# A DiT block with gated attention and 32 experts: unread products at the start, a reordered opening and attention step, smaller last transfers

## The chip, the cores and the metric

The kernel runs on one core of one Trainium2 chip. The metric is the device time of one launch in microseconds, as the median of several runs. Every operand and result is 32-bit float; a matrix product of such operands is two instructions on TensorE, a transposition is one.

## The reference

One transformer block over 256 tokens of width 1024, with 256 context tokens:

```python
sh1, sc1, g1, sh2, sc2, g2 = split(silu(c) @ w_mod + b_mod, 6)
h  = rms_norm(x, norm1_g) * (1 + sc1) + sh1          # and the same for ctx: keys and values only
k_a, v_a, k_b, v_b, q_a, q_b, g_a, g_b = split(h @ w_in)
y_a = global_attn(rope(q_a), [k_a, k_ctx], [v_a, v_ctx])
y_b = window_attn(rope(q_b), [k_b, k_ctx], [v_b, v_ctx], sink)
x = x + g1 * ((sigmoid(g_a) * (y_a @ w_br_a) + sigmoid(g_b) * (y_b @ w_br_b)) @ w_o)
h2 = rms_norm(x, norm2_g) * (1 + sc2) + sh2
top 4 of 32 experts a token, softmax weights "combine"
x = x + g2 * sum_e combine[:, e] * (swiglu(h2 @ w_e1[e] + b_e1[e]) @ w_e2[e] + b_e2[e])
out = rms_norm(x, final_g)
```

## The kernel before

**Weights.** All weights come through one queue of transfers that SyncE issues in the order of the list `pieces` (lines 45 to 86), into a ring of slots: four areas of 4 MB (`twins`), each two areas of 2 MB, each two halves of 1 MB. `pump` (line 99) issues the next pieces as long as a slot of their size is free, strictly in the list's order, and `done` (line 141) gives a slot back when the program has written its last use; on the chip SyncE then waits for the engine that reads it. Later `grow` adds a 4 MB area (`xxp`, line 638) and a 2 MB area (`r_qt`, line 820). Expert e has 8 MB in `w1` and 4 MB in `w2`. Experts 0 to 9 (`N_ONE = 10`) and 31 are loaded in 2 MB pieces, the others in 4 MB ones. The last two experts' second matrices are loaded together by output columns (`w2l`: three pieces of 2 MB and two of 1 MB).

**Opening (lines 184 to 335).** x is held transposed, 8 blocks of 128 features by 256 tokens. VectorE and ScalarE square the blocks, and TensorE sums the squares over the features by products with `ones` into `ssp` (line 232). `m0_prod(j)` computes block j of the first two modulation vectors as a row for c and one for c_ctx, and ScalarE copies it to `msb`; `m0_turn(j)` turns it into a column and VectorE modulates block j of x with it. `crow_half(h)` spreads half of silu(c) over all partitions (`cps`, tag "y", one buffer, which `ssp` uses too) for the rest of the modulation, which VectorE (`mod_v`) or GpSimd and ScalarE (`mod_p`, `mod_a`) compute as row sums. `inv_norm` is the root on ScalarE and the reciprocal on VectorE. Then, block by block, the q products (`q_prods`, line 296) run with the remaining modulation blocks between them.

**Attention (lines 511 to 636).** Eight units u (four of either branch, each two heads), in two halves `qt` of 128 tokens. The loop at line 611 writes the order of the engines' work by hand: transposition of the probabilities of unit u (`turn`, whose copies go to ScalarE and VectorE in turn), scores and exponentials of unit u + 1 (`scores`), the pending y steps, the product of the weights with the values of unit u - 1 (`weigh`, in the first half only), half a gate block, and a row or two of the modulation. `weigh` writes y and the spread row sums in one bank with one buffer; `y_steps` copies the row sums (ScalarE, line 578) and multiplies (VectorE, line 579). The steps that `weigh(u - 1)` leaves in the first half are thus done in the second half, behind the scores.

**From attention to the experts (lines 642 to 843).** The branch products and the output projection (`wo`, eight blocks m) on TensorE, with statistics, router logits and the experts' first bias prepared beside them. ScalarE then issues two transfers: g2 spread over the partitions (512 KB from a row in memory that was written before) and the second bias `be2` (256 KB). `x1_back(tb)` brings the new x back to tokens by features by products with the identity into `acc`, in which the experts' outputs are summed later. VectorE selects the top 4 and ranks the tokens of each expert; `pick` makes the selection matrix of a pair of experts.

**Experts (lines 847 to 1013).** At most 64 tokens an expert, two experts a pair. `gather` fetches the tokens of a pair by products, `gemm1` multiplies eight row blocks k of w1, `act` and `act_turn` form the activation, `gemm2` the eight blocks of w2, `scatter` adds the pair's outputs to `acc`. The loop at line 1002 runs the first `n` row blocks of expert e + 1, then `gemm2(e)`, then the other blocks. `steps` hangs small work into `gemm1` behind a given block: the gather of the next pair behind block 3 of each odd expert.

**End (lines 1015 to 1109).** Experts 30 and 31 are finished together by column groups: `last2(c)`, `share(c - 1)`, squares and `gain`. `total(tb)` sums the squares of a half of the tokens and takes the root on ScalarE, `finish(tb)` scales on ScalarE and VectorE and issues the output.

Of the kernel before, what the change touches and what calls it, by code (L numbers as in the profile page):

```python
# [7 lines left out]
F32 = mybir.dt.float32  # L8
# [7 lines left out]
DRAM = bass.MemoryType.DRAM  # L16

NE = 32
N_ONE = 10
CAP = 64  # L20
EPS = 1e-6
ALPHA = 1.702
# [13 lines left out]
def tile_dit_block(ctx: ExitStack, tc: tile.TileContext, xcT, consts, small, rows,  # L36
# [14 lines left out]
        pieces.extend(("mod", i, w_mod[i]) for i in ids)  # L51

    def w1s(e, ks):
        if ks in ((0, 1), (2, 3)) and e >= N_ONE:
            pieces.append(("w1", (e, ks[0]), w1[e, ks[0] // 2]))
        else:
            pieces.extend(("w1", (e, k), w1[e, k // 2, :, 4096 * (k % 2):4096 * (k % 2) + 4096]) for k in ks)

    def w2s(e):
        if e < N_ONE:  # L60
            pieces.extend(("w2", (e, k), w2[e, :, 4096 * k:4096 * k + 4096]) for k in range(2))
        else:
            pieces.append(("w2", (e, 0), w2[e]))
# [11 lines left out]
    pieces.extend(("wo", i, w_o[i]) for i in range(4))  # L75
    w1s(0, range(4))
    for e in range(NE - 2):
        n = 2 if e + 1 >= N_ONE else 1
        w1s(e + 1, tuple(range(n)))
        w2s(e)  # L80
        w1s(e + 1, tuple(range(n, 4)))
# [140 lines left out]
        return f1.tile([128, 256], F32, name=name, tag="t1", bufs=5)  # L222

    ssp = ps1.tile([128, 512], F32, name="ssp", tag="y")
    for k in range(8):
        sq = t1("sq")
        v = x[:, k, :]
        if k in (0, 1, 2, 5, 7):
            nc.vector.tensor_tensor(out=sq, in0=v, in1=v, op=ALU.mult)
        else:  # L230
            nc.scalar.activation(out=sq, in_=v, func=AF.Square)
        nc.tensor.matmul(ssp[:, 0:256], ones, sq, start=(k == 0), stop=(k == 7))

    def inv_norm(ps):
        r = t1("rinv")
        nc.scalar.activation(out=r, in_=ps, func=AF.Sqrt, bias=eps, scale=1.0 / 1024)
        nc.vector.reciprocal(r, r)
        return r
# [31 lines left out]

    def crow_half(h):

        cps = ps1.tile([128, 512], F32, name="cps", tag="y")
        for b in range(4):
            nc.tensor.matmul(cps[:, 128 * b:128 * b + 128],
                             cmod[:, 4 * h + b, 0:1].to_broadcast([128, 128]), ident, start=True, stop=True)
        nc.scalar.copy(out=crow[:, 512 * h:512 * h + 512], in_=cps)

    m0_prod(0)
    rinv = inv_norm(ssp[:, 0:256])  # L280
    m0_prod(1)
    crow_half(0)
    crow_half(1)
    for k in range(8):
        v = x[:, k, :]
        (nc.gpsimd if k >= 6 else nc.vector).tensor_tensor(out=v, in0=v, in1=rinv, op=ALU.mult)
        if k in (0, 2):
            m0_turn(k // 2)

    qa = [ps1.tile([128, 4, 256], F32, name="qa", tag="s", bufs=2) for _ in range(2)]  # L290
    csq = [tanh[2 + i // 2].rearrange("p a b -> p (a b)")[:, 512 * (i % 2):512 * (i % 2) + 512] for i in range(4)]
# [318 lines left out]

    for u in range(8):
        for qt in range(2):
            turn(u, 2 * qt)
            turn(u, 2 * qt + 1)
            if u < 7:
                scores(u + 1, qt)
            y_steps()
            if u and qt == 0:
                weigh(u - 1)
            if u < 7:  # L620
                gate_half(9 + u, qt)
            else:
                for m in (2 * qt, 2 * qt + 1):
                    tag, bufs = (("mm", 1), ("s", 2))[m % 2]
                    br_prod(0, m, ps1.tile([128, 512], F32, name="mm", tag=tag, bufs=bufs))
            if u < 7:
                norm_p(u + 1, qt)
            mod_v()
            if qt == 0 and u < 7:
                mod_p()  # L630
            elif u < 7:
                mod_a()
# [96 lines left out]
    braw = t8[1]  # L729
    b1e = b1.rearrange("(e c) n -> e (c n)", c=4)  # L730
    LOW_R, MID_R, ALL_R = slice(96, 128), slice(64, 96), slice(64, 128)
    for r in (slice(0, 32), MID_R, LOW_R):
        nc.scalar.dma_start(out=braw[r, :], in_=b1e)

# [14 lines left out]
    for m in range(8):  # L749
# [15 lines left out]
            stats(*pend)  # L765
        pend = (m, zt)
        bias_parts(m)
        if m == 1:

            ws = mtx[:, 3, :].rearrange("p (k e) -> p k e", k=8)  # L770
            nc.vector.tensor_tensor(out=ws, in0=wr, in1=sh2.unsqueeze(2).to_broadcast([128, 8, 32]), op=ALU.mult)
            for n in (4, 2, 1):
                nc.vector.tensor_tensor(out=ws[:, 0:n, :], in0=ws[:, 0:n, :], in1=ws[:, n:2 * n, :], op=ALU.add)
        elif m == 2:
            lp = ps2.tile([128, 512], F32, name="lp", tag="sp", bufs=2)
            nc.tensor.matmul(lp[:, 0:32], ones, ws[:, 0, :], start=True, stop=True)
            nc.vector.tensor_tensor(out=lb, in0=lp[:, 0:32], in1=brb, op=ALU.add)
    squares(sqs)
    stats(*pend)
    nc.scalar.dma_start(out=g2, in_=g2_dram[0:1, :].to_broadcast([128, 1024]))  # L780

    x_t, y_t = t8[0].rearrange("p (a c) -> p a c", a=2), [t8[1].rearrange("p (a c) -> p a c", a=2)]
    be2 = y_t[0][:, 1, 0:512]
    nc.scalar.dma_start(out=be2, in_=b2)

    nc.scalar.activation(out=junk, in_=eps, func=AF.Exp)
    acc = {}
# [1 line left out]
    def x1_back(tb):  # L789

        for h in range(2):
            acc[tb, h] = ps2.tile([128, 512], F32, name="acc", tag=("xg", "sp")[tb], bufs=2)
            for b in range(4):
                nc.tensor.matmul(acc[tb, h][:, 128 * b:128 * b + 128], x1T[:, 4 * h + b, 128 * tb:128 * tb + 128],
                                 ident, start=(b == 0), stop=False, skip_group_check=True)

    x1_back(0)
    nc.vector.reciprocal(rt, rt)
# [82 lines left out]
    def gemm1(e, u, ks, between=None):  # L881
        p, j = divmod(e, 2)
        for k in ks:
            if e == NE - 1 and k > 5:
                w = take("l1", k - 6)
            else:
                big = ("w1", (e, 2 * (k // 4) if N_ONE <= e < NE - 1 else k // 2))
                o = 2048 * (k % 4 if N_ONE <= e < NE - 1 else k % 2)
                w = take(*big)[:, o:o + 2048]
            for ch in (0, 2, 1, 3):  # L890
                c0 = 64 * (ch // 2)
                nc.tensor.matmul(u[c0:c0 + 64, ch % 2, :], XT[p][:, k, 64 * j:64 * j + 64],  # L892
                                 w[:, 512 * ch:512 * ch + 512], start=(e == 0 and k == 0), stop=(e > 0 and k == 7))
            if e == NE - 1 and k > 5:
                done("l1", k - 6)
            elif k % (4 if N_ONE <= e < NE - 1 else 2) == (3 if N_ONE <= e < NE - 1 else 1):
                done(*big)
            if between and k in between:
                between[k]()
# [29 lines left out]
    def gemm2(e, aT):  # L929
        p, j = divmod(e, 2)  # L930
        y = ps2.tile([128, 512], F32, name="y", tag="y")
        for k in range(8):
            n = 4 if e < N_ONE else 8
            w = take("w2", (e, k // n)).rearrange("p (k c) -> p k c", k=n)[:, k % n, :]
            l = aT[:, k % 4, 64 * (k // 4):64 * (k // 4) + 64]
            for h in range(2):
# [45 lines left out]
    def steps(e):  # L982
# [9 lines left out]
                s[5] = lambda: pick(p + 1)  # L992
            return s
        if e == 1:
            return {3: lambda: gather(p + 1), 6: settle}
        return {3: lambda: gather(p + 1)}

    u0 = ps2.tile([128, 2, 512], F32, name="u", tag="u")
    gemm1(0, u0, range(8), steps(0))
# [2 lines left out]
    for e in range(NE - 2):  # L1002
# [1 line left out]
        if p:  # L1004
            scatter(p - 1, (j,))
        u = bias1(e + 1)
        n = 4 if N_ONE <= e + 1 < NE - 1 else 2
        gemm1(e + 1, u, (0,))
        aT = act_turn(e)
        gemm1(e + 1, u, range(1, n), steps(e + 1))  # L1010
# [93 lines left out]
    total(0)  # L1104
    square(3, 1, False)
    square(4, 1, False)
    finish(0)
    total(1)
    finish(1)


# [182 lines left out]
```

## Time and profile before

| | us |
|---|---|
| median of 3 runs | 1190.56 |
| lowest, highest run | 1188.13, 1192.37 |
| the profiled execution, whole | 1187.26 |
| its span in the trace | 1185.5 |
| TensorE busy | 1108.2 |
| VectorE busy | 324.8 |
| ScalarE busy | 143.6 |
| GpSimd busy | 48.0 |

Times in the trace are from the start of the span; 1.8 us of the profiled execution lie around it. 456.88 MB are read from memory, 386 GB/s over the span. TensorE's products are pipelined and their ends are modelled, so a busy TensorE is not one at its peak. The row of an engine in order of time names start, duration, engine, line, operation, output, inputs and shapes; in brackets is how long the engine stood idle before it and what released it.

### The profile page before, as it was taken

What the parts mean: (1) busy time and instruction counts of PE and PEld (TensorE: products, weight loads), DVE (VectorE), ACT (ScalarE), POOL (GpSimd) and SP (SyncE); (2) the same over time, 40 slices, a digit from 0 to 9 for tenths busy, and PEclk for the clock granted to TensorE, in tenths of its full rate; (3) what the DMA queues carried; (4) which work ended last, traced back from release to release, by engine and by line L of the source; (5) the groups of instructions that cost most, each with busy time, mean ns of one, the idle gap of its engine ahead of it and who ended that gap; (6) DMA issues with size and microseconds to landing.
All of it is one profiled execution on the core that took longest, in us unless ns stands there. A gap on an engine that the chain in (4) does not pass through costs nothing.

```text
span 1185.5 us, 13010 instructions
## 1 busy us (share of the span) xinstructions
PE 1108.2 (93%) x5610; PEld 528.0 (45%) x5610; DVE 324.8 (27%) x711; ACT 143.6 (12%) x313; POOL 48.0 (4%) x37
## 2 busy tenths in 40 slices
PE   7999999999999999999999998989898989898986
PEld 5888666894334334343333333333333333333224
DVE  3273666343222221221212112121212121212123
ACT  2122554031000000000000000000000000000002
POOL 0232100030000000000000000000000000000001
PEclk9999999999999999999999999999999999999998
DMA  9995643959999999999999999999999999999994
GB/s 377 380 399 206 221 141 143 392 181 398 429 427 429 427 428 428 427 434 431 427 435 430 427 435 431 431 431 427 434 432 428 434 427 434 431 430 432 427 425 177
DMA packets 28735, 458.83 MB, mean 387 GB/s; under 512 B 3609, under 2 KB 4001, under 8 KB 6049
## 3 DMA queue, kind: packets, MB, share of 16 engines
q1 hardware_dynamic: 26928, 454.05, 90.9%
q10 hardware_dynamic: 1744, 3.90, 1.0%
q8 instruction: 46, 0.75, 0.3%
q14 instruction: 17, 0.13, 0.0%
HBM read 456.88 MB, written 1.05 MB: 386 GB/s over the span
## 4 chain that ended last, share of the span: by engine, by line
PE 59%; DMA 34%; DVE 4%; ACT 2%; issue 1%; ACTq 0%; DVEq 0%
DMA ring<-w 27%; PE u L892 24%; PE y L937 8%; DMA xxp<-w 7%; PE mm L395 3%; PE xg L855 3%; PE qa L296 2%; PE acc L953 2%; PE o L753 2%; PE br L599 2%; ACT xxp L537 1%; PE yl L1047 1%; PE kp L385 1%; PE vp L469 1%; PE ta L925 1%; DVE st L527 1%
## 5 line engine op out<-in xcount | busy, mean ns | idle before, releaser
L892 PE MATMUL u<-ring,t 128*64 128x512 f32 x1552 | 354.0, 602 | 22.2 <-DMA ring<-w 22.1
L892 PEld LDWEIGHTS u<-ring,t 128*64 128x64 f32 x1552 | 108.2, 138 | 231.6 <-issue 193.7
L937 PE MATMUL y<-ring,tmp 128*64 128x512 f32 x768 | 169.9, 594 | 17.3 <-DMA ring<-w 11.0
L944 DVE TENSOR_TENSOR t<-y,r_kv 64x512 f32<-64x512 f32 x60 | 41.3, 688 | 334.2 <-PE y L937 333.6
L937 PEld LDWEIGHTS y<-ring,tmp 128*64 128x64 f32 x768 | 53.6, 137 | 120.9 <-issue 100.1
L892 PE MATMUL u<-xxp,t 128*64 128x512 f32 x416 | 96.9, 613 | 5.4 <-DMA xxp<-w 5.4
L909 ACT ACTIVATE tmp<-tmp 128x512 f32<-128x512 f32 (+1 forms) x33 | 20.3, 617 | 629.0 <-DVE tmp L908 629.0
L908 DVE TENSOR_SCALAR tmp<-u 128x512 f32<-128x512 f32 (+1 forms) x33 | 22.3, 675 | 227.8 <-PE u L892 215.9
L855 PEld LDWEIGHTS xg<-r_kv,r_y 128*128 128x128 f32 x512 | 58.4, 192 | 12.2 <-issue 12.2
L855 PE MATMUL xg<-r_kv,r_y 128*128 128x128 f32 x512 | 61.3, 278 | 0.0
L395 PE MATMUL mm<-xxp,ring 128*128 128x256 f32 x256 | 59.9, 385 | 0.0
L953 PE MATMUL acc<-t,r_kv 128*128 128x512 f32 x120 | 59.5, 618 | 0.0
L857 DVE TENSOR_TENSOR t<-xg,modb 128x512 f32<-128x512 f32 x32 | 22.1, 691 | 132.9 <-PE xg L855 132.9
L892 PEld LDWEIGHTS u<-xxp,t 128*64 128x64 f32 x416 | 29.3, 140 | 63.5 <-issue 53.0
L395 PEld LDWEIGHTS mm<-xxp,ring 128*128 128x128 f32 x256 | 47.3, 190 | 12.6 <-issue 5.0
L937 PE MATMUL y<-xxp,tmp 128*64 128x512 f32 x176 | 39.0, 594 | 4.7 <-DMA xxp<-w 3.1
L1071 POOL TENSOR_TENSOR ring<-ring 128x256 f32<-128x256 f32 (+1 forms) x8 | 5.1, 660 | 894.4 <-DMA ring<-rows 892.7
L953 PEld LDWEIGHTS acc<-t,r_kv 128*128 128x128 f32 x120 | 20.3, 189 | 38.7 <-issue 38.7
L296 PE MATMUL qa<-xxp,ring 128*128 128x256 f32 x128 | 30.7, 388 | 0.0
L926 ACT COPY tmp<-ta 128x512 f32<-128x512 f32 x30 | 17.6, 585 | 103.5 <-PE ta L925 103.5
L753 PE MATMUL o<-r_qt,ring 128*128 128x256 f32 x128 | 28.9, 380 | 0.0
L353 DVE SCALAR_TENSOR_TENSOR ring<-ring,crow 128x1024 f32<-128x1024 f32 x22 | 26.3, 1211 | 0.0
(237 smaller groups left out, 852.7 us busy)
## 6 DMA issues: line engine op xcount, KB each, us to landing
ring<-w SPq DMA_DIRECT2D x49, 4096.0 KB, 40.4
ring<-w SPq DMA_DIRECT2D x47, 2048.0 KB, 18.5
xxp<-w SPq DMA_DIRECT2D x13, 4096.0 KB, 40.7
xxp<-w SPq DMA_DIRECT2D x10, 2048.0 KB, 16.5
ring<-w_mod SPq DMA_DIRECT2D x16, 1024.0 KB, 10.7
r_qt<-w SPq DMA_DIRECT2D x6, 2048.0 KB, 21.5
ring<-w_in SPq DMA_DIRECT2D x10, 1024.0 KB, 8.5
ring<-w_m SPq DMA_DIRECT2D x8, 1024.0 KB, 12.4
```

What stands on the lines that cost most here:

```text
L296: nc.tensor.matmul(qa[c // 4][:, c % 4, :], w[:, 128 * c:128 * c + 128], x[:, j, :], start=(j == 0 and c % 2 == 0), stop=(j == 7), skip_gr ...
L353: nc.vector.scalar_tensor_tensor(out=w, in0=w, scalar=1.0, in1=crow, op0=ALU.mult, op1=ALU.mult, accum_out=moda[:, t:t + 1])
L395: nc.tensor.matmul(gp[0][:, 0:256], w[:, k, :], x[:, k, :], start=(k == 0), stop=(k == 7))
L599: nc.tensor.matmul(ps[:, 0:256], w[:, k, 128 * (m % 2):128 * (m % 2) + 128], Y[:, 4 * br + k, :], start=(k == 0), stop=(k == 3))
L753: nc.tensor.matmul(ps[:, 0:256], w[:, k, :], M[:, k, :], start=(k == 0), stop=(k == 7))
L855: nc.tensor.matmul(xp[:, b, :], z[:, tb, 128 * k:128 * k + 128], S[:, tb, :], start=(tb == 0), stop=(tb == 1))
L857: nc.vector.tensor_tensor(out=XT[p][:, 4 * h:4 * h + 4, :], in0=xp, in1=sh2[:, 4 * h:4 * h + 4].unsqueeze(2).to_broadcast([128, 4, 128]), ...
L892: nc.tensor.matmul(u[c0:c0 + 64, ch % 2, :], XT[p][:, k, 64 * j:64 * j + 64], w[:, 512 * ch:512 * ch + 512], start=(e == 0 and k == 0), st ...
L908: nc.vector.tensor_scalar(out=w(glu), in0=v[:, bs, 0, :], scalar1=LIMIT, scalar2=None, op0=ALU.min)
L937: nc.tensor.matmul(y[64 * h:64 * h + 64, :], l, w[:, 512 * h:512 * h + 512], start=(k == 0), stop=(k == 7))
L944: nc.vector.tensor_tensor(out=YY[p][64 * j:64 * j + 64, 512 * h:512 * h + 512], in0=y[64 * h:64 * h + 64, :], in1=g2[64 * h:64 * h + 64, 5 ...
L953: nc.tensor.matmul(acc[tb, h], t[:, tb, :], y[:, s], start=False, stop=False, skip_group_check=True)
```

## The change

It has eight parts. (1) Sixteen products of `ones` with itself, into columns of `ssp` that nobody reads, stand ahead of the sum of squares. (2) The root and the two halves of the condition's row are written ahead of the first and the second modulation block, the halves in the two banks that the q products use later (tag "s"), and block 1 is turned right behind block 0. (3) In attention the y steps stand at the head of a half instead of behind the scores. (4) g2 and `be2` are loaded behind output block 2, `be2` into a free part of `msc`. (5) `x1_back` uses transpositions instead of products with the identity. (6) The gather of the next pair stands behind row block 2 instead of 3. (7) Experts 29 to 31 are loaded in 2 MB pieces (`N_TWO = 29`), so that expert 29 and 30 have two blocks instead of four ahead of `gemm2`. (8) The second half's sum and root stand ahead of the first half's scaling.

```diff
-N_ONE = 10
+N_ONE, N_TWO = 10, 29
 ...
     def w1s(e, ks):
-        if ks in ((0, 1), (2, 3)) and e >= N_ONE:
+        if ks in ((0, 1), (2, 3)) and N_ONE <= e < N_TWO:
 ...
     def w2s(e):
-        if e < N_ONE:
+        if not N_ONE <= e < N_TWO:
 ...
-        n = 2 if e + 1 >= N_ONE else 1
+        n = 2 if N_ONE <= e + 1 < N_TWO else 1
 ...
     ssp = ps1.tile([128, 512], F32, name="ssp", tag="y")
+
+    for _ in range(16):
+        nc.tensor.matmul(ssp[:, 256:384], ones, ones, start=True, stop=True)
 ...
-        cps = ps1.tile([128, 512], F32, name="cps", tag="y")
+        cps = ps1.tile([128, 4, 256], F32, name="cps", tag="s", bufs=2).rearrange("p a b -> p (a b)")[:, 0:512]
 ...
+    rinv = inv_norm(ssp[:, 0:256])
+    crow_half(0)
     m0_prod(0)
-    rinv = inv_norm(ssp[:, 0:256])
+    crow_half(1)
     m0_prod(1)
-    crow_half(0)
-    crow_half(1)
     for k in range(8):
         v = x[:, k, :]
         (nc.gpsimd if k >= 6 else nc.vector).tensor_tensor(out=v, in0=v, in1=rinv, op=ALU.mult)
-        if k in (0, 2):
-            m0_turn(k // 2)
+        if k < 2:
+            m0_turn(k)
 ...
         for qt in range(2):
+
+            y_steps()
             turn(u, 2 * qt)
             turn(u, 2 * qt + 1)
             if u < 7:
                 scores(u + 1, qt)
-            y_steps()
 ...
+    be2 = msc[:, 1:3, :].rearrange("p a b -> p (a b)")
 ...
         bias_parts(m)
+        if m == 2:
+            nc.scalar.dma_start(out=g2, in_=g2_dram[0:1, :].to_broadcast([128, 1024]))
+
+            nc.scalar.dma_start(out=be2, in_=b2)
 ...
-    nc.scalar.dma_start(out=g2, in_=g2_dram[0:1, :].to_broadcast([128, 1024]))
-
 ...
-    be2 = y_t[0][:, 1, 0:512]
-    nc.scalar.dma_start(out=be2, in_=b2)
 ...
-                                 ident, start=(b == 0), stop=False, skip_group_check=True)
+                                 ident, start=(b == 0), stop=False, is_transpose=True, skip_group_check=True)
 ...
-                big = ("w1", (e, 2 * (k // 4) if N_ONE <= e < NE - 1 else k // 2))
+                big = ("w1", (e, 2 * (k // 4) if N_ONE <= e < N_TWO else k // 2))
 ...
-        n = 4 if N_ONE <= e + 1 < NE - 1 else 2
+        n = 4 if N_ONE <= e + 1 < N_TWO else 2
 ...
-            return {3: lambda: gather(p + 1), 6: settle}
-        return {3: lambda: gather(p + 1)}
+            return {2: lambda: gather(p + 1), 6: settle}
+        return {2: lambda: gather(p + 1)}
 ...
+    total(1)
     finish(0)
-    total(1)
     finish(1)
```

The lines left out repeat the same condition on e in `gemm1` and `gemm2`.

## Rows read from the trace of the kernel before

**Rows 1.** Table by stage: stretch, length, busy PE, PEld, DVE, ACT, POOL; clock, transfer share, GB/s.

```profile
88.00:98.00 10.00, 9.32 (x44) 7.89 (x43) 6.60 (x15) 1.58 (x3) 0.00 (x0) 1.00 0.01 2
246.00:256.00 10.00, 10.00 (x54) 8.97 (x53) 4.51 (x8) 4.35 (x7) 6.72 (x4) 1.00 0.08 34
282.00:561.00 279.00, 275.71 (x1332) 103.73 (x1328) 61.19 (x117) 15.22 (x27) 0.00 (x0) 1.00 1.01 428
561.00:1126.00 565.00, 517.98 (x2426) 191.64 (x2424) 108.59 (x210) 26.80 (x48) 0.00 (x0) 0.98 1.00 431
```

**Rows 2.** Chain of waits: start, length, what, one of its expert transfers.

```profile
561.47 39.73 DMA ring<-w
```

**Rows 3.** Table by stage for line 232 alone: TensorE's products and weight loads.

```profile
6.50:11.00 4.50, 4.41 (x10) 3.53 (x11) 1.00 1.02 430
11.00:12.60 1.60, 1.59 (x7) 1.07 (x5) 1.00 1.02 430
```

**Rows 4.** In order of time, the opening.

```profile
0.85 0.17 DVE L200 MEMSET ones<- 128x128 f32 x1 [0.85 <-PEq L1287]
...
6.59 6.01 PE L232 MATMUL ssp<-sq,ones 128*128 128x256 f32 x16 [6.59 <-DVE sq L229]
...
16.35 1.16 PE L275 MATMUL cps<-keep,cmod 128*128 128x128 f32 x8 [0.68 <-ACT crow L277]
...
19.65 1.99 PE L296 MATMUL qa<-xxp,ring 128*128 128x256 f32 x8
```

**Rows 5.** In order of time, the attention loop.

```profile
175.62 0.69 ACT L537 ACTIVATE xxp<-s,st 128x512 f32<-128x512 f32 x1 [3.09 <-DVE st L532]
...
177.45 0.43 DVE L579 TENSOR_TENSOR r_y<-y,r 128x256 f32<-128x256 f32 x1 [1.75 <-ACT r L578]
...
177.79 0.15 DVE L546 TENSOR_TENSOR st<-st 128x2 f32<-128x2 f32 x1
...
178.06 1.21 DVE L353 SCALAR_TENSOR_TENSOR ring<-ring,crow 128x1024 f32<-128x1024 f32 x1
...
181.32 0.69 ACT L537 ACTIVATE xxp<-s,st 128x512 f32<-128x512 f32 x1 [2.10 <-DVE st L532]
...
183.17 1.20 DVE L353 SCALAR_TENSOR_TENSOR ring<-ring,crow 128x1024 f32<-128x1024 f32 x1
...
196.81 1.04 PE L553 MATMUL tp<-keep,xxp 128*128 128x128 f32 x8
...
199.54 0.66 PE L569 MATMUL y<-keep,st 128*64 128x128 f32 x8 [1.69 <-DVE r_y L579]
```

**Rows 6.** In order of time, from the routing to the first gather.

```profile
269.09 2.03 PE L794 MATMUL acc<-keep,r_qt 128*128 128x128 f32 x16
...
269.59 0.98 DVE L831 TENSOR_SCALAR r_kv<-keep,rankm,rt 128x64 f32<-128x64 f32 x4
...
270.96 3.74 PE L855 MATMUL xg<-r_kv,r_y 128*128 128x128 f32 x32
```

**Rows 7.** Transfers issued at 256.69, 278.32 and 1128.91: size, us to landing.

```profile
ring<-w SPq DMA_DIRECT2D x1, 2048.0 KB, 7.1
...
ring<-w SPq DMA_DIRECT2D x1, 2048.0 KB, 8.3
...
ring<-w2l SPq DMA_DIRECT2D x1, 2048.0 KB, 34.3
```

**Rows 8.** In order of time, SyncE's and TensorE's last experts.

```profile
1128.89 7.09 PE L892 MATMUL u<-ring,t 128*64 128x512 f32 x32 [2.67 <-DMA ring<-w]
...
1128.91 5.22 SPq L135 DMA_DIRECT2D ring<-w2l  x2
...
1165.03 3.67 PE L1047 MATMUL yl<-ring,t 128*64 128x256 f32 x32
```

**Rows 9.** In order of time, the last scaling.

```profile
1177.75 0.34 DVE L1086 SCALAR_TENSOR_TENSOR ring<-ring,fin 128x128 f32<-128x128 f32 x1
...
1178.96 0.72 ACT L1083 ACTIVATE ring<-ring,fin 128x512 f32<-128x512 f32 x1 [0.29 <-DVE fin L1082]
```

More of the change, by code (lines that the diff above doesn't have):

```diff
@@ L886, in gemm1 @@
             else:
-                big = ("w1", (e, 2 * (k // 4) if N_ONE <= e < NE - 1 else k // 2))
-                o = 2048 * (k % 4 if N_ONE <= e < NE - 1 else k % 2)
+                big = ("w1", (e, 2 * (k // 4) if N_ONE <= e < N_TWO else k // 2))
+                o = 2048 * (k % 4 if N_ONE <= e < N_TWO else k % 2)
                 w = take(*big)[:, o:o + 2048]
@@ L895, in gemm1 @@
                 done("l1", k - 6)
-            elif k % (4 if N_ONE <= e < NE - 1 else 2) == (3 if N_ONE <= e < NE - 1 else 1):
+            elif k % (4 if N_ONE <= e < N_TWO else 2) == (3 if N_ONE <= e < N_TWO else 1):
                 done(*big)
@@ L932, in gemm2 @@
         for k in range(8):
-            n = 4 if e < N_ONE else 8
+            n = 8 if N_ONE <= e < N_TWO else 4
             w = take("w2", (e, k // n)).rearrange("p (k c) -> p k c", k=n)[:, k % n, :]
```

## The prediction

> **What bounds the kernel now.** I read three views first. The table by stage [rows 1] shows where the transfers stand still: between 88 and 98 us and between 246 and 256 us the DMA share is 0.01 and 0.08, because the ring is full and waits for TensorE and VectorE to free slots. From 282 us on it is 1.00 without a break, at 428 and then 431 GB/s, to the last experts. The chain of waits [rows 2] says the same of the second part: from 561 us it is made of transfers of expert weights. So the program has two halves. Before 282 us the compute chain sets the pace, and what it saves moves the whole stream earlier. After it the bytes set the pace, and there only fewer bytes in that stretch, or a shorter way from the last bytes to the end, are worth anything. The third view, in order of time, shows each edited place [rows 3 to 8].
>
> **The start.** The eight products that sum the squares begin at 6.59 us and take 6.01 us for 16 instructions; the q products need 1.99 us for eight of the same width [rows 4]. Split at 11 us, ten of them need 4.41 us and seven, one of them counted twice, 1.59 us [rows 3], 0.44 against 0.23 each: the 1.2 GHz level and then the 2.4 GHz level by the spacing, although the granted-clock column says 1.00 in both. What TensorE did before the rise is work without a gap since 6.59 us. The change puts 16 unread 128-wide products, 32 instructions, ahead. Their operand is written at 0.85 to 1.02 us [rows 4], so they start at 1.1. At the high level one costs 0.127 us (2.03 us for 16 [rows 6]), at the low one I take twice that. If the rise comes after as much work as above, 4.5 us, 18 are done by 5.6 us and 14 more take 1.8 us: they end at 7.4, and the sum of squares starts 0.8 us late but takes 4.0 instead of 6.0 (0.25 an instruction, from the q products). Gain 2.0 - 0.8 = 1.2 us. Bounds: all 32 at the low level end at 9.2 us, 2.6 us late, with nothing won back; at best the full 2.0.
>
> The order behind it: the root for rinv no longer stands behind the copy of the first modulation product on ScalarE, and the second half of the condition's row no longer waits 0.68 us for its buffer [rows 4]. The chain to the first q product at 19.65 us is otherwise the same TensorE work, so I take 0.6 us, and bounds of 0 and 0.7. The turn at k = 1 instead of 2 moves one VectorE multiplication behind it and has room. Start together: **1.8 us**, from -2.6 to 2.7.
>
> **Attention.** VectorE and ScalarE alternate there. In a half-step without y steps it is 1.85 us from the first exponential (181.32) to VectorE's modulation row (183.17); in one with them 2.44 us (175.62 to 178.06), since the copy of the row sums and the multiplication stand behind the exponentials [rows 5]. Moved to the head of the half-step they cost VectorE its 0.34 us (177.45 to the next start at 177.79; the row's 0.43 overlaps it) and no wait. So 2.44 - 1.85 - 0.34 = 0.25 us a head, six of them 1.5 us. The copy now stands ahead of the next transposition's copy on ScalarE and could stall it if the product it reads were late. It is not: that product is queued before the gate's products, and ScalarE comes to it only after two exponentials. Then TensorE's idle 1.69 us before the last-but-one weighing product at 199.54 (released by the multiplication) goes, since that multiplication is done a half-step earlier; the transpositions end at 197.85 [rows 5], and from there the chain is TensorE's own products, up to the routing. **3.2 us**, from 0 (TensorE bound at the same pace) to 6 x 0.59 + 1.69 = 5.2.
>
> **Into the experts.** The eight products that bring x1 back take 2.03 us in 16 instructions; eight transpositions of the same size take 1.04 us [rows 5, 6]. The first set lies beside VectorE's routing steps. The second ends a microsecond earlier, but the gather that follows reads the selection that VectorE ends at 270.57, against its start at 270.96 [rows 6]. **0.4 us**, bounds 0 and 1.0; late next is the selection.
>
> The two transfers (512 and 256 KB) that ScalarE issues at 267 us run beside the stream's first pieces. Moved to m = 2 they are issued while ScalarE waits for the next output block, hidden behind that block's eight products on TensorE (uncovered, only that block's square would come late, and its sums are taken one block later), and their bytes fall into the empty stretch from 246 to 256 us [rows 1]. A 2 MB piece alone lands after 7.1 us; the one issued at 278.32, behind them, after 8.3 [rows 7]. From there the stream has no break. **1.2 us**, bounds 0 and 1.8 (0.79 MB at 428 GB/s).
>
> The gather at k = 2 instead of 3 puts a product between it and the second GEMM. Both are TensorE time in the half that the bytes bound: nothing, and if that cover went, TensorE's short wait there would show in each odd expert. A freed slot comes one gather, 3.74 us [rows 6], later, against transfers issued some 40 us ahead [rows 2].
>
> **The last experts.** Expert 29's and 30's weights come as 2 MB pieces, so the last four row blocks of expert 30 needn't wait for the whole 4 MB: half of 7.09 us, 3.5 us, leaves TensorE's chain after 1128.89 [rows 8]. But the third piece of the last weights is issued at 1128.91 and lands 34.3 us later, at 1163.2 [rows 7, 8]; its product starts at 1165.03. So 1.8 us, and late next is that landing. Against it: 2 MB pieces ran at 428 GB/s, 4 MB ones at 431 [rows 1], 0.7% of 88 us (three experts of 12.6 MB), 0.6 us. **1.2 us**, from -0.6 to 3.5. The Trainium skill ("DMA: Bandwidth & Descriptors", section "Anatomy of one DMA") speaks against this part: it gives every transfer a fixed cost of some 2 us. By it, as an estimate, five more transfers would cost 10 us instead of 0.6, and the sum would be a loss of 1.3. The trace does not agree for transfers in a full queue.
>
> The second root ahead of the first scaling: between the end of the first scaling on VectorE (1178.09) and the second on ScalarE (1178.96) stand a sum, two small steps and the root [rows 9]; they move beside the first, which they push back by 0.3. **0.3 us**, bounds 0 and 0.5.
>
> **Sum:** 1.8 + 3.2 + 0.4 + 1.2 + 1.2 + 0.3 = 8.1 us. Against the profiled execution's 1187.26 that is 1179.2. The median of the runs shown is 1190.56, 3.3 above it, and the runs after are compared with such runs: **1182.5 us**. The ends of all bounds add to -3.2 and 14.7.
>
> **Rivals.** (1) The front shrinks by half: the products end no earlier than the clock's rise can pay for (0.6 left at the start) and TensorE takes VectorE's place in attention (1.0 left). Then 0.6 + 1.0 + 0.4 + 1.2 + 1.2 + 0.3 = 4.7, 1185.9. For it: apart from that one gap no row shows how far TensorE stands behind VectorE there. Against it: the gap is its longest, and it goes. Chance 0.20.
>
> (2) The stream doesn't follow the front: slots come free earlier, but the bytes from 0 to 83 us were the limit. Then 1.2 + 1.2 + 0.3 = 2.7, 1187.9, no change that counts. Against it stand the two empty stretches [rows 1], behind which any earlier start is taken up. 0.10.
>
> (3) Slower: with halved pieces the queue runs dry in the last three experts, since a piece must wait for the one small area that an earlier piece still holds. Ten pieces at 7.1 us alone [rows 7] instead of five at 9.7 (4.19 MB at 431 GB/s [rows 1]) are 22 us more: 1182.5 + 1.2 + 22 = 1205.7. It decides once a slot comes free later than what is queued lasts; transfers are issued some 40 us ahead [rows 2], so it needs a wait of that length, and a slower kernel needs 9 us of dryness. 0.04. The Trainium skill's fixed cost, of the same page and section, would act in the same place; by it alone the time would be some 1191.9 us.
>
> (4) That products without a reader are left out of the program: only 0.6 remains of the start, 1183.7, inside the forecast's spread; 0.03.
>
> **How the numbers follow.** The forecast has 0.61, for gains from 5.5 to 12. About 0.3%, 3.6 us, is what a measurement of this kernel can tell from no change. Forecast, (1) and (4) are faster: 0.84. (2) is the same, with some scatter: 0.11. Slower 0.05: (3) and what I have not seen. The range goes from the forecast's better end, 1177.0, to rival (2) at 1188.0.
>
> **What would show it.** Right: the squares' products 0.25 apart from their first, ending near 11.4; the first q product near 17.9; no wait for the multiplication before the weighing products; expert 0's first product 5.4 us earlier; the third of the last pieces landing just before its product. Wrong: a first q product after 19.6, 2.44 us still from exponential to modulation row, pauses in the transfers after 1070, or transfers whose share falls below 1.00 between 282 and 1126 us.

## The result, and the profile after

The changed kernel takes 1179.71 us (median of four runs, 1178.89 to 1181.75) against 1190.75 us (four runs): the ratio is 0.9919, with an interval of 0.9900 to 0.9939. It is faster by 0.8%, a small change but clear of that interval, 2.8 us below the forecast of 1182.5 and inside the range of 1177.0 to 1188.0. Its profiled execution, however, was its longest, 1181.75 us with a span of 1179.9, while that of before was one of the shortest, so the two traces differ by only 5.6 us. A second profile of the same kernel (label again, below) has a span of 1178.1. The first trace shows what went wrong on the way, and the second is the better measure of the parts.

The start and the attention loop in the first profile, TensorE in order of time:

```profile
1.07 5.56 PE L227 MATMUL ssp<-ones 128*128 128x128 f32 x32 [1.07 <-DVE ones L200]
6.50 3.72 PE L235 MATMUL ssp<-sq,ones 128*128 128x256 f32 x16
...
16.59 1.99 PE L299 MATMUL qa<-xxp,ring 128*128 128x256 f32 x8
...
183.14 0.66 PE L572 MATMUL y<-keep,st 128*64 128x128 f32 x8
...
192.40 0.66 PE L572 MATMUL y<-keep,st 128*64 128x128 f32 x8
...
195.07 3.29 PE L602 MATMUL mm<-r_y,ring 128*128 128x256 f32 x14 [0.28 <-ACT t L400]
```

The squares take 3.72 us instead of 6.01 and are not late, and the first q product comes 3.06 us earlier than at 19.65 [rows 4]. The y products no longer wait for VectorE's multiplication, as the one at 199.54 did for 1.69 us [rows 5]. When the output projection begins, at 226.30 instead of 233.08, the lead is 6.8 us. But the first expert's first product starts at 271.15 instead of 274.62, a lead of 3.5. Between them lies this stretch of the output projection, of the same trace:

```profile
234.58 1.96 POOL L743 CAST be<-t 32x2048 bf16<-32x2048 f32 x1 [26.41 <-DMA t<-b]
234.72 2.11 DVE L780 TENSOR_TENSOR t<-r_kv,modb 128x256 f32<-128x256 f32 x1
...
236.86 2.61 DVE L782 TENSOR_TENSOR t<-t 128x128 f32<-128x128 f32 x3
...
239.52 0.41 PE L785 MATMUL lp<-t,ones 128*128 128x32 f32 x2 [1.47 <-DVE t L782]
...
239.77 5.39 PE L758 MATMUL o<-r_qt,ring 128*128 128x256 f32 x16
```

VectorE's product of the router's weights started 0.14 us after a conversion on GpSimd and took 2.11 us, where it took 0.42 before the change. TensorE waited 1.47 us for its sums at the lp product (which only prepares the router's bias), and the 16 instructions of the next output block, 3.62 us elsewhere, took 5.39. The table by stage of the same trace (stretch, length, busy PE, PEld, DVE, ACT, POOL; granted clock, transfer share, GB/s) tells why:

```profile
239.50:240.50 1.00, 0.98 (x5) 0.87 (x6) 0.81 (x3) 0.54 (x2) 0.00 (x0) 0.86 0.28 115
240.50:242.00 1.50, 1.50 (x5) 1.19 (x4) 0.43 (x2) 1.18 (x2) 0.22 (x1) 0.50 0.49 175
242.00:245.00 3.00, 3.00 (x12) 2.50 (x11) 0.00 (x0) 0.00 (x0) 1.90 (x1) 0.73 0.49 178
```

The granted clock fell to 0.50, the 1.2 GHz level, behind the wait. The wait (1.47) and the slower products (5.39 - 3.62 = 1.77) are 3.2 of the 3.3 us by which the lead shrank (6.78 to 3.47).

The end of the first profile, in order of time:

```profile
1160.20 3.67 PE L1052 MATMUL yl<-ring,t 128*64 128x256 f32 x32 [0.20 <-DMA ring<-w2l]
...
1173.58 0.34 SPq L1093 DMA_DIRECT2D out<-ring  x1
...
1174.44 0.35 ACTq L1093 DMA_DIRECT2D out<-ring  x1
```

The third of the last weight pieces is what its product waits for, as forecast; before, the product came 1.8 us behind the landing [rows 7, 8]. The outputs leave 0.86 us apart instead of 1.58 (1178.24 and 1179.82 before).

### The profile page after: what moved, and what is told of

The parts are those of the page before. It is cut to its first block, busy times and chain, and to the rows that moved or that the text cites. A ratio compares the mean times of both kernels' runs of the same rounds, so it can differ in the third digit from the quotient of the medians.

```text
span 1179.9 us, 13059 instructions
## 1 busy us (share of the span) xinstructions
PE 1112.7 (94%) x5626; PEld 531.6 (45%) x5626; DVE 326.6 (28%) x711; ACT 143.3 (12%) x313; POOL 47.4 (4%) x37
## 4 chain that ended last, share of the span: by engine, by line
PE 61%; DMA 35%; DVE 1%; issue 1%; ACT 1%; ACTq 0%; SPq 0%; DVEq 0%
PE u L897 22%; DMA ring<-w 20%; DMA xxp<-w 9%; PE y L942 8%; PE xg L860 5%; PE mm L398 5%; DMA r_qt<-w 3%; DMA ring<-w2l 3%; PE qa L299 2%; PE acc L958 2%; PE o L758 2%; PE br L602 2%; PE s L522 1%; PE kp L388 1%; PE vp L472 1%; PE tp L556 1%
## 5 line engine op out<-in xcount | busy, mean ns | idle before, releaser
L897 PE MATMUL u<-xxp,t 128*64 128x512 f32 x400 | 94.3, 615 | 6.5 <-DMA xxp<-w 6.5
L758 PEld LDWEIGHTS o<-r_qt,ring 128*128 128x128 f32 x128 | 25.0, 199 | 3.5
```

What stands on the lines that cost most here:

```text
L758: nc.tensor.matmul(ps[:, 0:256], w[:, k, :], M[:, k, :], start=(k == 0), stop=(k == 7))
```

## The experiments

Twelve runs with eleven kernels (one of them is timed twice, and one is the changed kernel itself). Each was timed beside the kernel before, whose medians were 1188.2 to 1189.1 us in the five groups. Differences are against `ws_early`, unless another kernel is named.

**1. The changed kernel again, and the router's product one block earlier.** `again` is unchanged. `ws_early`:

```diff
-        if m == 1:
+        if m == 0:
             ws = mtx[:, 3, :].rearrange("p (k e) -> p k e", k=8)
```

> The changed kernel as it stands, for a second profile. In its first profile 3.4 us of the 6.8 us that the front had gained were gone by the end of the output projection: VectorE's product of the router's weights took 2.11 us beside GpSimd's conversion of the bias rows (0.42 us before the change), TensorE waited 1.47 us for it, and the granted clock of the next 3 us was 0.50. Theory A: which of the two engines starts first there is a matter of 0.1 us (GpSimd began 0.14 us ahead here, at the same moment before), so it can differ from one run to the next. Where it does not happen, the output projection starts and ends with the same lead, the first expert's first product comes near 268 us instead of 271.15, and the whole is near 1178.5 us. Theory B: the change causes it in every run (the lead of the front, or the two transfers now issued in the middle of this stage). Then the second profile shows the wait of about 1.5 us at the lp product again, the first expert's first product near 271, and the whole near 1180 to 1182.

> The changed kernel with VectorE's product of the router's weights and its three additions one block earlier in the output projection (block 0 instead of block 1), when GpSimd's first conversion has not begun. Theory A and B for the cause of the wait alike: no wait of TensorE at the lp product, the granted clock stays 1.00 through the stage, the lead of 6.8 us at its start is kept to its end, and the first expert's first product comes near 267.8 us. If the front's lead reaches the end one for one, the whole is 3 us below a run that has the wait (1178.5 against 1181.7). Rival (a lead gained before the experts is lost in the weight stream): the first expert's first product comes earlier and the third of the last weight pieces lands no earlier than at 1160.0, the whole stays within 1 us of the changed kernel.

`again` took 1179.65 us (1178.45 to 1179.92; ratio 0.9909, 0.9891 to 0.9928), `ws_early` 1178.58 (1178.30 to 1179.49; 0.9906, 0.9887 to 0.9924). The trace of `again` in order of time:

```profile
235.07 0.42 DVE L780 TENSOR_TENSOR t<-r_kv,modb 128x256 f32<-128x256 f32 x1
235.52 2.35 DVE L782 TENSOR_TENSOR t<-t 128x128 f32<-128x128 f32 x3
235.65 1.90 POOL L743 CAST be<-t 32x2048 bf16<-32x2048 f32 x1 [27.13 <-DMA t<-b]
...
238.24 0.31 PE L785 MATMUL lp<-t,ones 128*128 128x32 f32 x2
...
268.07 10.52 PE L897 MATMUL u<-ring,t 128*64 128x512 f32 x48
...
1157.21 3.67 PE L1052 MATMUL yl<-ring,t 128*64 128x256 f32 x32 [0.16 <-DMA ring<-w2l]
...
1171.46 0.35 ACTq L1093 DMA_DIRECT2D out<-ring  x1
```

The bias rows landed later, so GpSimd started 0.58 us behind VectorE's product instead of 0.14 ahead; TensorE did not wait, and the clock was 1.00. Theory A holds: the change does not cause the wait in every run. The two engines stood as near to each other before the change, where they began in the same hundredth of a microsecond:

```profile
241.50 0.42 DVE L771 TENSOR_TENSOR t<-r_kv,modb 128x256 f32<-128x256 f32 x1
241.50 2.16 POOL L738 CAST be<-t 32x2048 bf16<-32x2048 f32 x1 [26.55 <-DMA t<-b]
```

Which of them comes first can thus differ from run to run in either kernel; how often it is GpSimd is not shown.

In `again` the lead of 6.43 us at the output projection (226.65) is still 6.55 at the first expert and 8.36 at the last output (1179.82 to 1171.46). `ws_early` keeps its lead in the same way (1171.27); its median is 1.1 us lower, with ranges that overlap.

**2. `ws_early` a second time**, beside experiments 6 to 8.

> The version ws_early unchanged, a second time, beside the next three on the same chip. Expected if the wait at the lp product is really out of it: granted clock 1.00 through the output projection, the first expert's first product near 267.9 us, a median within 0.7 us of 1178.6. If the wait can still happen, some of the runs lie 2 to 3 us higher.

1179.37 us (1178.34 to 1181.23), the first expert at 267.77. Two of the six runs are near 1181.2: something else costs some runs 2 us, and no profile caught it. So `ws_early` removes one known wait, but that it beats the changed kernel (1179.71 and 1179.65) is not shown. The same kernel's median moved by 0.8 us from one group to the other, so below a difference of medians against `ws_early` (1178.58) is good to about that, and the traces are the better measure.

**3. Parts of the start undone, each from `ws_early`.** `no_products`, then `order_old`, then `half_products`:

```diff
-    for _ in range(16):
-        nc.tensor.matmul(ssp[:, 256:384], ones, ones, start=True, stop=True)
```

```diff
-    rinv = inv_norm(ssp[:, 0:256])
-    crow_half(0)
     m0_prod(0)
-    crow_half(1)
+    rinv = inv_norm(ssp[:, 0:256])
     m0_prod(1)
+    crow_half(0)
+    crow_half(1)
```

```diff
-    for _ in range(16):
+    for _ in range(8):
```

(`order_old` also has the row's old buffer and the second turn at k = 2.)

> The version with the router's product moved one block up (ws_early, 1178.58 us), without the 16 unread products. My theory (they bring TensorE's rise to the 2.4 GHz level forward, out of the sum of squares): the squares' 16 instructions take about 6.0 us from 6.5 instead of 3.72 from 6.64, the first q product comes about 2.4 us later than at 16.73, near 19.1, and everything after it is later by the same amount; the whole 2.0 to 2.4 us longer, near 1180.9. Rival (the gain at the start comes from the order of the work behind the squares alone): the first q product comes within 0.5 us of 16.73 and the whole does not change.

> The version ws_early with the order behind the sum of squares as it was before the change: both modulation blocks' products around the root, the condition's rows after them in the small buffer, the second turn at k = 2. My theory: the first q product comes 0.3 to 0.7 us later than at 16.73, the unread products still bring the squares' 3.72 us, and the whole is 0.6 us longer, 1179.2, at the edge of what can be told. Rival (the order is worth most of the 2.9 us that the start gained): the first q product near 19, the whole 2 us longer.

> The version ws_early with 8 unread products in place of 16. From the rows: unread instructions ran about 0.25 us apart up to some 4.1 us and 0.127 apart after it, so 16 instructions end near 4.8 us, and TensorE stands still from there to the first square at 6.6. [...] Theory B (the level falls again in the gap, as it fell to 0.50 in the output projection after 1.5 us without work): the squares take between 4.5 and 6 us, the first q product comes 0.8 to 2.3 us later than at 16.73, the whole 1179.4 to 1181.

1180.74, 1180.67 and 1180.47 us. TensorE in order of time, first in `no_products`:

```profile
6.36 6.46 PE L233 MATMUL ssp<-sq,ones 128*128 128x256 f32 x16 [6.36 <-DVE sq L230]
...
19.19 1.99 PE L297 MATMUL qa<-xxp,ring 128*128 128x256 f32 x8
```

in `order_old`:

```profile
6.51 3.72 PE L235 MATMUL ssp<-sq,ones 128*128 128x256 f32 x16
...
11.95 1.07 PE L258 MATMUL mp<-ring,cmod 128*32 128x256 f32 x16 [0.72 <-DMA ring<-w_m]
...
18.08 1.99 PE L299 MATMUL qa<-xxp,ring 128*128 128x256 f32 x8
```

and in `half_products`:

```profile
1.06 3.78 PE L227 MATMUL ssp<-ones 128*128 128x128 f32 x16 [1.06 <-DVE ones L200]
6.52 5.25 PE L235 MATMUL ssp<-sq,ones 128*128 128x256 f32 x16 [1.67 <-DVE sq L232]
...
18.14 1.99 PE L299 MATMUL qa<-xxp,ring 128*128 128x256 f32 x8
```

The unread products are worth 2.46 us (19.19 against 16.73), and the whole follows: the last output leaves 2.94 us later (1174.21 against 1171.27). Of that, 0.65 us arises between the output projection and the first expert, where the granted clock of this trace read 0.50 from 265 to 267 us. The median is 2.2 us above `ws_early`'s and 1.4 above `ws_again`'s. The order is worth 1.35 us beside the products, more than expected: with the squares done early, the old order stands for 0.72 us at the second modulation block, which has not landed yet. Its median is 2.1 us up, but its last output leaves only 1.20 us later, at 1172.47. Without the products the order is worth only what is left of the start's 2.92 us (19.65 to 16.73), 0.46.

Eight products are not enough: TensorE stands still for 1.67 us behind them and the squares take 5.25 us, so 1.41 us of the gain is lost. These are theory B's sizes, but its ground, that the level falls again in the gap, is not shown. The table of line 227 (duration of one instruction in ns: least, median, most; first and last start) says that there was nothing to fall from, first in `half_products` and then in `ws_early`:

```profile
L227 PE MATMUL ssp<-ones x16: 421/421/582, 1.1 to 4.4; 128*128 128x128 f32 x16
...
L227 PE MATMUL ssp<-ones x32: 275/275/582, 1.1 to 6.0; 128*128 128x128 f32 x32
```

None of the 16 instructions of the eight products was of the short kind that makes up most of the 32 in `ws_early`: they ended before the rise. By the spacing the rise comes at 4.0 us in `ws_early`, near 4.7 in the first profile and near 5.6 in `again`, so it differs between runs. The granted-clock column says 1.00 in all of it.

**4. The y steps behind the scores again** (`attn_old`, from `ws_early`).

```diff
-            y_steps()
             turn(u, 2 * qt)
             turn(u, 2 * qt + 1)
             if u < 7:
                 scores(u + 1, qt)
+            y_steps()
```

> The version ws_early with the steps on the attention's row sums after the scores again, not at the head of the half-step. My theory: the stretch from the first q product (16.73) to the first output projection (226.47) becomes 3.7 us longer, with the wait of 1.7 us for VectorE's multiplication before the weighing near 199 back and the rest in six half-steps of about 0.3 us each; everything after it is later by 3.7 us, the whole near 1182.3. Rival 1 (TensorE is the bound in attention in this version, the steps' place matters only at the end): 1.7 us longer, 1180.3. Rival 2 (the stream takes the lead back): the lead is lost up to the first expert, the whole within 1 us of 1178.6.

1182.38 us (1182.01 to 1183.42), 3.8 us more than `ws_early` and 3.0 more than `ws_again`. TensorE's rows of the y products with a wait, in order of time:

```profile
142.91 0.66 PE L572 MATMUL y<-keep,st 128*64 128x128 f32 x8 [1.26 <-DVE r_y L582]
153.53 0.66 PE L572 MATMUL y<-keep,st 128*64 128x128 f32 x8 [0.31 <-DVE r_y L582]
164.15 0.66 PE L572 MATMUL y<-keep,st 128*64 128x128 f32 x8 [0.23 <-DVE r_y L582]
174.96 0.66 PE L572 MATMUL y<-keep,st 128*64 128x128 f32 x8 [0.42 <-DVE r_y L582]
185.78 0.66 PE L572 MATMUL y<-keep,st 128*64 128x128 f32 x8 [0.42 <-DVE r_y L582]
196.59 0.66 PE L572 MATMUL y<-keep,st 128*64 128x128 f32 x8 [1.70 <-DVE r_y L582]
```

The output projection starts at 230.13 instead of 226.47, 3.66 us later, and the last output leaves at 1174.79 instead of 1171.27, 3.52 us later. My theory holds, and the lead arrives almost whole at the end. With the steps at the head the y products show no wait, and the chain of waits of `ws_early` and `again` runs almost over TensorE alone from 110 to 187 us, where in `before` and `attn_old` it alternates with VectorE and ScalarE: TensorE has become the bound there.

**5. g2 and `be2` transferred behind the output projection** (`g2_old`, from `ws_early`).

```diff
-        if m == 2:
-            nc.scalar.dma_start(out=g2, in_=g2_dram[0:1, :].to_broadcast([128, 1024]))
-            nc.scalar.dma_start(out=be2, in_=b2)
...
     stats(*pend)
+    nc.scalar.dma_start(out=g2, in_=g2_dram[0:1, :].to_broadcast([128, 1024]))
+    nc.scalar.dma_start(out=be2, in_=b2)
```

> The version ws_early with the two transfers of 512 and 256 KB issued after the output projection again instead of at its block 2. My theory: the front up to the first expert's first product (267.89) keeps its time, the two transfers push back the expert weights behind them, and the third of the last pieces lands 0.8 to 1.8 us later than at about 1157; the whole 1.2 us longer, near 1179.8. Rival (the stream is not full yet when they run, the bytes fit in): the third of the last pieces lands at the same time within 0.3 us, and the whole does not change.

1179.68 us (1179.12 to 1181.04), 1.1 us above `ws_early` and 0.3 above `ws_again`. The trace gives the smaller value: the third piece's product starts at 1157.49 instead of 1157.02, and 0.11 us of that is there at the first expert (268.00 against 267.89). 0.36 us is left. TensorE's table by stage (stretch, length, busy, granted clock, transfer share, GB/s) has the reason, in `g2_old`:

```profile
270.00:276.00 6.00, 6.00 (x30) 1.00 0.91 352
```

and in `ws_early`:

```profile
270.00:276.00 6.00, 6.00 (x30) 1.00 0.62 221
```

The stream waits for a slot there (SyncE issues nothing between 264.1 and 271.5 us in either trace), and the two transfers' bytes mostly run in time that is otherwise empty. The rival is nearer.

**6. The last experts in 4 MB pieces** (`pairs_old`, from `ws_early`).

```diff
-N_ONE, N_TWO = 10, 29
+N_ONE, N_TWO = 10, 31
```

> The version ws_early with the last experts' weights in 4 MB pieces again (N_TWO = 31). My theory: row blocks 4 to 7 of expert 30 wait for the whole piece, TensorE's chain after it ends later, the third of the last pieces is no longer what its product waits for (it lands about 1156.5, 0.6 us earlier by the faster pieces, and its product starts 1.8 us after that), and the whole is 1.2 us longer, near 1179.8. Rival 1 (the term was too large since landing sets the end in either version): the product of the third piece starts within 0.5 us of 1157.0, the whole unchanged. Rival 2 (2 MB pieces cost the stream more than they give): the whole shorter by 1 us.

1180.68 us (1179.80 to 1182.90), 1.3 us above `ws_again` in the same group: the theory's size. In order of time, and then its table by stage:

```profile
1122.35 8.57 PE L897 MATMUL u<-ring,t 128*64 128x512 f32 x32 [2.62 <-DMA ring<-w]
...
1159.97 3.67 PE L1052 MATMUL yl<-ring,t 128*64 128x256 f32 x32
```

```profile
1119.50:1122.30 2.80, 0.23 (x2) 0.94 0.91 386
1122.30:1125.00 2.70, 2.65 (x8) 0.50 1.01 431
```

The product waits 2.62 us for its piece and then runs its first part at the 1.2 GHz level: 8.57 us instead of the 7.09 that the same product took behind the same wait before [rows 8]. Two of the six runs, the profiled one among them, took 1182.6 and 1182.9 us, the others 1179.8 to 1181.2; that the fall alone sets them apart is likely and was not tried. In this trace the third piece's product starts 3.2 us later than in `ws_again` (1159.97 against 1156.77), and 1.5 us of that is the fall. With the smaller pieces the longest wait at this place is 1.25 us. The Trainium skill ("DMA: Bandwidth & Descriptors", section "Anatomy of one DMA"), which the prediction cites for every transfer, gives a fixed cost of about 2 us for a transfer on GpSimd's path; SyncE issues these. Carried over to them, and added up one transfer after the other, five transfers fewer would be an estimated 10 us shorter. The runs do not agree.

**7. 4 MB pieces from expert 6 on** (`n_one6`, from `ws_early`; `N_ONE = 6`).

> The version ws_early with 4 MB pieces from expert 6 on instead of expert 10 (N_ONE = 6). If bytes are the limit from the first experts on, four experts of 12.6 MB go at 431 instead of 428 GB/s: 0.8 us less, 1177.8. If TensorE is the limit there (its busy share is 0.99 from 296 to 557 us) the larger pieces make it wait for whole ones and the whole is the same or 1 to 5 us longer.

1183.36 us (1181.70 to 1184.40), 4.0 above `ws_again`: larger pieces are no gain where TensorE needs them at once. TensorE's busy time between 480 and 557 us falls from 77.00 to 74.88 us, with a wait of 2.0 us for a piece in `xxp`, and the last pieces' first product comes at 1151.39 instead of 1147.60 in `ws_again`.

**8. The two engines' meeting, forced** (`forced` and `forced_two`, from the changed kernel).

```diff
+        if m == 1:
+            for _ in range(2):
+                nc.gpsimd.tensor_tensor(out=tmp4[:, 2, :], in0=mtx[:, 1:3, :].rearrange("p a b -> p (a b)"),
+                                        in1=mtx[:, 1:3, :].rearrange("p a b -> p (a b)"), op=ALU.mult)
```

This is `forced_two` (it reads both blocks of `zt`), with GpSimd's first conversion moved behind it. `forced` has three operations of half the width and the conversion in its place.

> The changed kernel with three unread two-input operations of 128x256 on GpSimd, about 0.63 us each, behind VectorE's scaling in block 1 of the output projection, so that GpSimd is at work when VectorE comes to the two-input operations ahead of the lp product, in every run. Theory A (a two-input operation of VectorE beside GpSimd is held up until GpSimd ends, TensorE waits for it and its granted clock falls): VectorE's addition and its product of the router's weights, 0.42 us each alone, take over 1.5 us more together, TensorE waits 1.4 us or more at the lp product, the granted clock behind it shows values between 0.5 and 0.9, the first expert's first product comes at 270.5 to 272 us instead of 268.07, and the whole is 1.5 to 3.5 us above the changed kernel's, near 1182. Rival (the 2.11 us in the first profile came from something else, such as the bias rows' transfer): VectorE's operations keep 0.42 us, the product starts without a wait, the whole stays near 1179.5.

> The changed kernel with two unread two-input operations of 128x512 on GpSimd (about 1.25 us each) behind VectorE's scaling in block 1 of the output projection, and GpSimd's first conversion of the bias rows behind them in its queue instead of ahead, so that GpSimd begins just before VectorE comes to the router's product. In the run forced the conversion stood ahead of the added operations and they ran five microseconds too late. Theory A (VectorE is held up while GpSimd works, TensorE waits for it at the lp product, and its granted clock can fall behind the wait): VectorE's addition, product and three sums take over 1.5 us longer than the 0.43 + 0.42 + 2.35 us of the second profile, TensorE waits 1 us or more at the lp product, and the first expert's first product comes 1 to 4 us after 268.07; 1180.5 to 1183 as a whole. Rival (the 2.11 us of the first profile came from something else): the lp product starts without a wait, first expert near 268.0, the whole near 1179.5.

`forced` took 1180.44 us and decides nothing on the lp product: the added operations stood behind the conversion in GpSimd's queue and ran from 240.16, and the first expert starts at 267.93. It shows a one-input operation held as well: VectorE's scaling at 238.32 took 1.92 us beside GpSimd, 0.35 elsewhere. `forced_two` took 1184.06 us, five of its runs between 1183.7 and 1184.7 and one at 1180.34. In order of time, and by stage:

```profile
234.42 2.43 POOL L767 TENSOR_TENSOR tmp<-t 128x512 f32<-128x512 f32 x2 [26.28 <-DVE t L764]
234.69 1.26 DVE L784 TENSOR_TENSOR t<-r_kv,modb 128x256 f32<-128x256 f32 x1
...
235.99 5.00 DVE L786 TENSOR_TENSOR t<-t 128x128 f32<-128x128 f32 x3
...
241.04 0.64 PE L789 MATMUL lp<-t,ones 128*128 128x32 f32 x2 [3.01 <-DVE t L786]
...
241.49 6.40 PE L758 MATMUL o<-r_qt,ring 128*128 128x256 f32 x16
```

```profile
240.00:241.00 1.00, 0.00 (x0) 0.00 (x0) 1.00 (x2) 0.00 (x0) 0.94 (x1) 0.57 0.04 16
241.00:243.00 2.00, 1.96 (x6) 1.69 (x7) 1.26 (x4) 1.50 (x3) 0.00 (x0) 0.50 0.18 29
```

Theory A holds, beyond the sizes that I gave, and the granted clock fell before the wait was over: 3.0 us of wait and 2.8 us more for the block behind it (6.40 against 3.62) put the first expert at 273.87, 5.80 us later than in `again`. The whole is 4.4 us longer than `again`'s. The Trainium skill ("SBUF — State Buffer", section "SBUF: two separate sides") says that VectorE and GpSimd share a pair of ports under an exclusive lock, and that whichever starts first has it for its whole instruction; for VectorE this concerns operations with two inputs in SBUF (against a GpSimd operation that reads it) and those in a two-port mode. The rows agree: 2.11 us when GpSimd was 0.14 us ahead, 0.42 when it was not.

## Why the prediction came out as it did

The sum was 8.1 us; from the trace of before to that of `again` the last output leaves 8.36 us earlier. That they agree so well is partly luck: the start, the attention and the finish gave 1.7 us more than forecast, the other terms 1.4 us less. The terms, against the rows:

- **Start**, forecast 1.8, measured 2.74 in `again` (19.65 to 16.91) and 3.06 in the first profile. The failed term is "0.8 us late" for the sum of squares: the unread products end at 6.3 to 7.2 us instead of 7.4, and the squares' own operands come at 6.4 to 6.6. The price of an instruction, 0.25 and 0.127 us, came from the length of a whole group; the rows show them about 0.22 us apart at first (16 between 1.1 and 4.4 us in `half_products`) and 0.11 later (20 in 2.19 us in `ws_early`). The squares then took 3.6 to 3.7 us, not 4.0. Hence 2.46 instead of 1.2 for the products. For the order I took 0.6; it was 0.46 alone and 1.35 beside the products.
- **Attention**, forecast 3.2, measured 3.7 (again 3.69, `attn_old` 3.73). The gap of 1.69 us goes as forecast. The six heads were read from VectorE's chain at 0.25 us each; the limit was TensorE's wait for the same multiplication, which `attn_old` shows at 1.26 us in the first unit, 0.2 to 0.4 in the next four and 1.70 in the last. In the trace of before its six waits add up to 4.3 us, so 0.6 of them were not won.
- **x1 back**, forecast 0.4, measured 0.12 (6.55 against 6.43 of lead). The transpositions take half the time, but the chain goes through the selection, as I named as late next.
- **g2 and be2**, forecast 1.2, measured about 0.4. The step that failed is that the two transfers push back the piece issued at 278.32 [rows 7] and all behind it. SyncE had issued nothing since 271.5 us in that trace, and the stream has a break just ahead of the stretch that I read as unbroken from 282. The row of before, with the columns of [rows 1], has a transfer share of 0.66:

```profile
278.00:280.00 2.00, 2.00 (x12) 0.72 (x10) 0.00 (x0) 0.00 (x0) 0.00 (x0) 1.00 0.66 156
```

After the change the same break comes at 270 to 274 us.
- **The last experts**, forecast 1.2. The third piece's product lost its 1.8 us behind the landing, and `pairs_old` is 1.3 us longer. Between before and `again` this term and the last one together brought 1.27 us (the product's lead of 7.82, 1165.03 to 1157.21, less the 6.55 at the first expert), not 2.4; with 0.4 for the transfers 0.9 is left for the last experts. The 0.6 us against it was counted for three whole experts; only five pieces of 4 MB are split, at the same rates 0.3.
- **Finish**, forecast 0.3, measured 0.54: from the last scatter product to the last issue 3.86 us (1167.60 to 1171.46) instead of 4.40 (1175.42 to 1179.82).

**The rivals.** The halved front of rival (1) is what the first profile has at the first expert (3.5 of 6.8 us), but by a mechanism that I did not name; TensorE did take VectorE's place in attention and cost nothing. Rival (2) falls: `attn_old` and `no_products` move the last output by 3.52 and 2.94 us where they move the first expert by 3.67 and 3.07. Rival (3) falls: no pause in the transfers, 427 GB/s from 1037 to 1122 us. Rival (4) falls: the products are in the trace.

**The distance of 2.8 us** between the forecast and the median is not in the sum. I set it against 1190.56, the median of three runs; eleven runs of before gave 1189.03, from 1187.9 to 1194.2, and the same sum from there is 1180.9. The rest, about 1 us, is not in any pair of traces. Before scatters more than the changed kernel's second group, and chance waits like the one found here may be part of it; that was not tried. The range has a slip of its own: the largest gain that I gave, 12 us, ends at 1178.6, not at 1177.0.

## What to carry to other kernels

Read a lead at several places along the trace, not at the ends alone: where it shrinks, something new stands there, here two engines that met by 0.1 us. A short wait of TensorE can cost twice, once as the wait and once as the slower products behind it, where TensorE sets the pace; so small work that TensorE waits for belongs well ahead of its use and away from GpSimd's operations. A transfer moved out of a full stream is worth its bytes only if the stream is full at that very place.

## What the runs showed of the hardware that I had not expected

- The granted clock fell to 0.50 at TensorE waits of 1.47, 2.62 and 3.01 us inside long busy stretches, behind the first and towards the end of the others, and the products behind them took 1.8, 1.5 and 2.8 us more. At a wait of 2.67 us at the same product of the last experts it stayed at 1.00 before the change [rows 8]. Even within one trace, waits of one length do and do not cost the clock; TensorE in `again`, where the granted clock fell to 0.50 behind the first of these two waits and stayed at 1.00 behind the second:

```profile
653.09 8.79 PE L897 MATMUL u<-xxp,t 128*64 128x512 f32 x32 [2.62 <-DMA xxp<-w]
...
771.21 7.09 PE L897 MATMUL u<-ring,t 128*64 128x512 f32 x32 [2.63 <-DMA ring<-w]
```

- At the start the products' spacing shows the slow level (16 instructions of squares in 6.46 us against 3.72) while the granted clock reads 1.00.
- VectorE operations on SBUF alone that began shortly after one of GpSimd's took 1.3 to 2.2 us instead of 0.35 to 0.42, with one input (1.92 in `forced`) as with two (2.11 in the first profile). One that also reads TensorE's output was not held: 0.48 us at 242.12 in `again`, in the middle of GpSimd's work.
